# Adaptive-norm modulation in four column groups of TensorE, in plain float32

## The chip, the cores and the metric

One core of a Trainium2 chip runs the kernel. The metric is the device time of one execution in microseconds, the median over several runs. The profile is of one execution; its clock starts with the first instruction on the core.

## What is computed

The kernel is one inference step of a one-layer hybrid decoder: 1024 prompt positions and 8 sequences of 4 new positions, 1056 rows of width 1024. The part that is changed is the modulation, a small product of the 9 conditioning vectors (1 prompt, 8 samples) with a wide weight:

```python
mod = (jax.nn.silu(c) @ p['w_mod'] + p['b_mod'])[:, None, :]
sh_m, sc_m, g_m, sh_f, sc_f, g_f = jnp.split(mod, 6, axis=-1)
h = rmsnorm(x, p['g_pre_mix']) * (1.0 + sc_m) + sh_m
z = h @ p['w_in']
...
x = x + g_m * rmsnorm(merged @ p['w_out'], p['g_post_mix'])
hf = rmsnorm(x, p['g_pre_ffn']) * (1.0 + sc_f) + sh_f
```

`w_mod` is 1024 x 6144 in float32. The first third of `mod` (`sh_m`, `sc_m`) is needed before the first product `h @ w_in` can begin; the rest only after the branches (convolution, S5 state space, attention) have been merged.

## The kernel before, in words

All weights come from memory in float32. A large product is done three times in the fast format fp32r: each weight tile is split into a rounded part `whi` (ScalarE, L414) and a remainder `wlo` (VectorE, L415), the data likewise into `hh` and `hl`, and TensorE runs `whi*hh`, `whi*hl`, `wlo*hh`. Plain float32 operands need no split; TensorE then runs each matmul as two passes, which the trace shows as two MATMUL rows.

The order of the work is a list of atoms. An atom is a piece of TensorE work (for a 128-column weight tile: three atoms, one for each 352 of the 1056 rows, 24 matmuls each) with the weight units it needs, an assumed cost in microseconds, and an evacuation of PSUM that is issued after the next atom's matmuls. `run` (L370) walks over the list. Before an atom it issues splits (`split`, L397) of the units that `ready` lets through, and loads (`load`, L382) up to three units ahead. `Side` (L218) holds generators for the work beside the products (convolution taps on VectorE, attention, the sample's attention, layer norm, S5). After each atom `side.advance(cost)` lets every generator go on by that cost, so the generators' instructions stand between the atoms according to assumed costs and not to measured time. `side.finish` and `side.drain` issue whatever is left of a generator at once, with no atom between.

The modulation is cut into 12 column blocks `n` of 512 columns, each into 4 units `kk` of 128 x (2 x 512) weights (512 KB).

- Blocks 0 to 3 are made first (`first_mod`, L540): 16 units through 6 buffers `mw`, two plain float32 matmuls a unit with a stationary of 9 columns (`cs1`) and 512 moving columns. Block `n` is turned from rows to columns by `turn_mod` (4 transposes) while block `n+1` is running. Between these units, in TensorE's program order, stand the statistics of the first two thirds of `x` (`first_stats`: 4 matmuls of one column, then a Newton root on VectorE ending in `rs_dg`) and their broadcast (`first_norm`).
- Blocks 4 to 11 (32 units) are atoms among the products (`mod_atoms`, L568; `add_mod`, L599, cost 0.9). Their weights are split like all others. A unit has four fp32r matmuls of 18 stationary columns (`c18`, rounded part and remainder of the conditioning) by 512. At a block's end ScalarE copies 18 x 512 out of PSUM into a part of `vm` (L574), TensorE transposes it in four pieces (L576), VectorE adds the parts.

`some_mods(n)` puts the next `n` units into the list: one after each q and k tile, one after each conv half and gate tile, through the 11 tiles up to and after the S5 input.

In attention `value` (L849) multiplies by head with output in partitions 0 to 63 or 64 to 127; its program order is pair, head, key block, so that with two key blocks two matmuls (four passes) for one head stand before two for the other. In S5 (`s5_gen`, L1260), for each of 4 quarters, `Gin` times `U` alternates matmul by matmul between the halves of the partitions; ScalarE copies the result `E`, VectorE scans it and builds `HP`, and TensorE multiplies `Tm` by `U` and `Go` by `HP`. When the list comes to `open_m(0)` (L1728), `side.finish` issues what is left of S5.

Of the kernel before, what the change touches and what calls it, by code (L numbers as in the profile page):

```python
# [8 lines left out]
F32 = mybir.dt.float32  # L9
# [41 lines left out]
V_CB, V_LG, V_LB, V_CW = 80, 84, 88, 92  # L51
NVEC = 92 + 124
C_ID, C_ONE = 0, 128
NCST = 256

# [16 lines left out]
def _constants():  # L74
    f = np.float32
    cst = np.zeros((128, NCST), f)
    cst[:, C_ID:C_ID + 128] = np.eye(128)
    cst[:, C_ONE:C_ONE + 128] = 1.0
    sel = np.zeros((12, 6, 128), f)
    for gp in range(6):  # L80
        for m in range(128):
            sel[4 * (gp // 2) + 2 * (gp % 2) + m // 64, gp, m] = 1.0
    slopes = np.exp2(f(-8.0) * np.arange(1, NSLOPE + 1, dtype=f) / f(NSLOPE)).astype(f)
    tab = np.full((128, 2560), BIG, f)
    qi = np.arange(128)[:, None]
    ki = np.arange(256)[None, :]
    dist = qi + 128 - ki
    ok = (dist >= 0) & (dist <= 128)
    for g in range(2):
        for h in range(4):  # L90
            t = slopes[4 * g + h] * (DIL[g] * dist).astype(f)
            tab[:, (4 * g + h) * 256:(4 * g + h + 1) * 256] = np.where(ok, t, f(BIG))
    i2 = np.arange(128)
    dist2 = i2[:, None] - i2[None, :]
    ok2 = (dist2 >= 0) & (dist2 % 2 == 0)
    for h in range(4):
        t = slopes[8 + h] * (8 * dist2).astype(f)
        tab[:, 2048 + h * 128:2048 + (h + 1) * 128] = np.where(ok2, t, f(BIG))
    smp = np.full((128, 992), BIG, f)
    for b in range(8):  # L100
        for h in range(4):
            for j in range(4):
                r = b * 16 + h * 4 + j
                m = np.arange(512)
                d = 512 + j - m
                smp[r, 0:512] = np.where((d % 4 == 0) & (d <= 512), slopes[4 + h] * d.astype(f), f(BIG))
                m = np.arange(128)
                d = 128 + j - m
                smp[r, 512:640] = np.where(d <= 128, slopes[h] * d.astype(f), f(BIG))
                m = (np.arange(64)[:, None] * 16 + np.arange(4)[None, :]).reshape(-1)  # L110
                d = 1024 + j - m
                smp[r, 640:896] = np.where(d % 16 == 0, slopes[8 + h] * d.astype(f), f(BIG))
                for g in range(3):
                    for j2 in range(4):
                        if j2 == j or (g == 0 and j2 < j):
                            smp[r, 896 + g * 32 + b * 4 + j2] = slopes[4 * g + h] * f(j - j2)
    return cst, sel, tab, smp
# [138 lines left out]
def program(tc, I, O):  # L256
# [113 lines left out]
    def run():  # L370
# [11 lines left out]
        def load(v):  # L382
            src, n, scale, op, keep = units[v]
            if op:
                op['load']()
                return
            raw = wp.tile([128, 1024], F32, tag="raw", name="raw")
            sp.dma_start(out=raw[:, 0:n], in_=src)
            raws[v] = raw
# [7 lines left out]
        def split(v):  # L397
            src, n, scale, op, keep = units[v]
            for t in tags(v):
                rings[t].append(v)  # L400
            if op:
                flush()
                if v + 1 < len(units) and units[v + 1][3]:
                    units[v + 1][3]['pre']()
                parts[v] = wp.tile([128, 1024], F32R, tag=tags(v)[0], name="wop")
                op['make'](parts[v])
                return
            raw = raws.pop(v)
            if keep:
                hi, lo = keep()  # L410
            else:
                hi = wp.tile([128, 1024], F32R, tag="whi", name="whi")
                lo = wp.tile([128, 1024], F32R, tag="wlo", name="wlo")
            act.activation(out=hi[:, 0:n], in_=raw[:, 0:n], func=AF.Copy, scale=scale)  # L414
            dve.scalar_tensor_tensor(out=lo[:, 0:n], in0=raw[:, 0:n], scalar=scale, in1=hi[:, 0:n].bitcast(F32),  # L415
                                     op0=ALU.mult, op1=ALU.subtract)
            parts[v] = (hi, lo)

        def ready(v, i):
            if any(len(rings[t]) >= 3 and last[rings[t][-3]] >= i for t in tags(v)):  # L420
                return False
            ahead = 6 if units[v][3] else 2
            return v < ahead or first[v - ahead] <= i

        def loadable():
# [76 lines left out]
    ks_ = sc_.tile([128, 3, 2, 32], F32, name="ks_")  # L502
    vm = sc_.tile([128, 768], F32, name="vm")
    vs_ = vm[0:32].rearrange("p (g x) -> p g x", g=3)
    mrow = vm[64:82, 0:512]
    cvp_, close_cv = open_pool("cv", side="right", bufs=1)
    mp, close_mp = open_pool("mp", side="right", bufs=1)
    cT = mp.tile([128, 8, 9], F32, name="cT")
# [22 lines left out]
    act.activation(out=cth, in_=cT, func=AF.Tanh, scale=0.5)  # L531
    cs2 = mp.tile([128, 8, 9], F32, name="cs2")
    dve.scalar_tensor_tensor(out=cs2, in0=cth, scalar=1.0, in1=cT, op0=ALU.add, op1=ALU.mult)
    c18 = sc_.tile([128, 8, 18], F32R, name="c18")
    act.activation(out=c18[:, :, 0:9], in_=cs2, func=AF.Copy)
    TT(c18[:, :, 9:18], cs2, c18[:, :, 0:9].bitcast(F32), ALU.subtract)
    cs1 = mp.tile([128, 8, 9], F32, name="cs1")
    dve.tensor_scalar(out=cs1, in0=cs2, scalar1=0.5, scalar2=None, op0=ALU.mult)

    def first_mod(n, kk):  # L540

        def emit(_):
            if kk == 0:
                mws['s', n] = zt()
            s = mws['s', n]
            i = 4 * n + kk
            w = mws.pop(i)
            for k2 in range(2):
                k = kk * 2 + k2
                mm(s[0:9, :], cs1[:, k, :], w[:, k2 * 512:(k2 + 1) * 512], k == 0, k == 7)  # L550
            load_mw(i + 6)
            if kk == 1 and n:
                turn_mod(n - 1)

        def finish(_):
            mws['row', n] = mp.tile([9, 512], F32, tag="row", name="row", bufs=2)
            act.activation(out=mws['row', n], in_=mws['s', n][0:9, :], func=AF.Copy)
        atoms.append(Atom([], 1.7, emit, finish if kk == 3 else None))

    def turn_mod(n):  # L560
        row = mws.pop(('row', n))
        s = mws.pop(('s', n))
        for i in range(4):
            pe.transpose(out=s[:, i * 9:(i + 1) * 9], in_=row[:, i * 128:(i + 1) * 128], identity=ident[0:9, 0:9])
        TT(mod[:, 4 * n:4 * n + 4, :], s[:, 0:36].rearrange("p (i x) -> p i x", i=4),
           vecs[:, V_BMOD + 4 * n:V_BMOD + 4 * n + 4].unsqueeze(2).to_broadcast([128, 4, 9]), ALU.add)

    def mod_atoms(n):  # L568

        box = {}  # L570

        def finish(_):
            s = box['s']
            act.activation(out=mrow, in_=s[0:18, :], func=AF.Copy)  # L574
            for i in range(4):
                pe.transpose(out=s[:, i * 18:(i + 1) * 18], in_=mrow[:, i * 128:(i + 1) * 128],  # L576
                             identity=ident[64:82, 64:82])
            t3 = s[:, 0:72].rearrange("p (i x) -> p i x", i=4)
            tm = sc_.tile([128, 4, 9], F32, tag="mtm", name="mtm", bufs=2)
            TT(tm, t3[:, :, 0:9],  # L580
               vecs[:, V_BMOD + 4 * n:V_BMOD + 4 * n + 4].unsqueeze(2).to_broadcast([128, 4, 9]), ALU.add)
            TT(mod[:, 4 * n:4 * n + 4, :], tm, t3[:, :, 9:18], ALU.add)

        out = []
        for kk in range(4):
            def emit(w, kk=kk):
                if kk == 0:
                    box['s'] = mt()
                s = box['s']
                hi, lo = w[0]  # L590
                for k2 in range(2):
                    k = kk * 2 + k2
                    mm(s[0:18, :], c18[:, k, :], hi[:, k2 * 512:(k2 + 1) * 512], k == 0, False)
                    mm(s[0:18, :], c18[:, k, :], lo[:, k2 * 512:(k2 + 1) * 512], False, k == 7)
                return None
            out.append((flat(I['wmod'][n, kk]), emit, finish if kk == 3 else None))
        return out

    def add_mod(m):  # L599
        if atoms[-1].tag == 'mod' and atoms[-1].evac:  # L600
            plain(lambda: None)
        u = unit(m[0], 1024, 0.5)
        atoms.append(Atom([u], 0.9, m[1], m[2], tag='mod'))

    hpool, close_h = open_pool("hpool", bufs=1)
    hh = hpool.tile([128, 8, T], F32R, name="hh")
# [499 lines left out]
    def s5_prep():  # L1106
# [73 lines left out]
        yield 2.0  # L1180
        tmp1, tmp2 = t16(), t16()

        PW = sc_.tile([128, 2, 9, 16], F32, name="PW")
        dve.memset(PW[:, 0, 0, :], 1.0)
        dve.memset(PW[:, 1, 0, :], 0.0)
        TT(PW[:, 0, 1, :], mag, co, ALU.mult)
# [41 lines left out]
        yield 2.0  # L1228
        cmul_small(5, 4, 4)

        WK = sc_.tile([128, 7, 2, 16], F32, name="WK")

        def csq(orr, oi, ar, ai):
            TT(tmp1, ai, ai, ALU.mult)
# [427 lines left out]
    for g in range(3):  # L1662
        for what, base, scale in (('Q', 12, -0.125), ('K', 18, 1.0)):
            for p in range(2):
                put(z_atoms(base + 2 * g + p, scale, qk_evac(g, what, p)))
                some_mods(1)
        if g == 0:
            conv_job(1, 1)
            conv_start(1)
# [2 lines left out]
        plain(lambda g=g: P_.update({('gen', g): side.add(att_gen(g))}))  # L1672
        if g < 2:
            conv_job(g + 2, 1)
        gate_jobs(GA[g], 1)
        if g < 2:
            conv_start(g + 2)
        plain(lambda: None)
        plain(lambda g=g: side.finish(P_['gen', g]))
    plain(lambda: (P_.update(cg=side.add(combine_gen())), side.add(s5_prep())))  # L1680
    gate_jobs(GC, 1)
    plain(lambda: (side.finish(P_['cg']), P_['close_ap'](), close_cv(), open_ub(), side.add(ln_gen()),
                   side.add(sample_gen())))
    gate_jobs(GS, 0)
# [737 lines left out]
```

## Time and profile before

| what | before |
|---|---|
| median of 3 runs | 1982.06 us (1979.92 to 1983.1) |
| the profiled execution | 1981.16 us |
| span of its instructions | 1979.4 us |
| TensorE busy | 1890.1 us, 95% |
| VectorE busy | 1339.0 us, 68% |
| ScalarE busy | 735.7 us, 37% |
| mean granted TensorE clock | 0.976 |

The span is the time from the first instruction on the core to the last; 1.8 us of the execution lie outside it. Busy time counts an engine's own instructions; matmuls overlap, and their ends are modelled, so what a matmul costs in a row of matmuls is read from the distance of starts.

### The profile page before, as it was taken

How to read it: one execution, taken by the hardware profiler on the slowest of the kernel's cores; microseconds unless marked ns; L12 is line 12 of the kernel's file. 1: busy time of each engine (PE TensorE's matmuls, PEld its weight loads, DVE VectorE, ACT ScalarE, POOL GpSimd, SP SyncE). 2: the span in 40 equal slices, each digit the busy share in tenths (PEclk: the TensorE clock that was granted, in tenths of full speed). 3: DMA queues.
4: the chain of work that ended last, by engine and by line, in shares of the span. 5: the costliest groups of instructions: out<-in, count | busy, mean ns of one | idle time of the engine just before them, and what ended most of it. 6: DMA issues, size and time to landing. Idle time of an engine off the chain costs nothing. (4 is left out here: it accounts for less than half of the span.)

```text
span 1979.4 us, 33713 instructions
## 1 busy us (share of the span) xinstructions
PE 1890.1 (95%) x13512; PEld 1761.9 (89%) x13512; DVE 1339.0 (68%) x2747; ACT 735.7 (37%) x1442; POOL 230.2 (12%) x385
## 2 busy tenths in 40 slices
PE   7999999999999899999899999999999999999995
PEld 2899799789777789999799999989999999999995
DVE  5777686465366676665596667777777777667686
ACT  3422422431531443222223446434333333464452
POOL 0000001001010023122200001100000000110123
PEclk9999999999999999999999999999999999999997
DMA  7333124224237453233852345541423223575654
GB/s 287 96 107 111 47 107 151 67 97 165 86 123 282 166 177 124 92 116 95 238 158 89 106 153 196 207 167 67 133 85 109 82 88 119 200 266 182 218 196 152
DMA packets 89261, 282.23 MB, mean 143 GB/s; under 512 B 16004, under 2 KB 22244, under 8 KB 86928
## 3 DMA queue, kind: packets, MB, share of 16 engines
q1 hardware_dynamic: 51824, 138.49, 21.6%
q0 software_dynamic: 29936, 115.11, 16.7%
q10 hardware_dynamic: 7344, 26.47, 4.0%
q8 instruction: 106, 1.74, 0.4%
q14 instruction: 51, 0.42, 0.1%
HBM read 212.80 MB, written 68.15 MB: 142 GB/s over the span
## 5 line engine op out<-in xcount | busy, mean ns | idle before, releaser
L307 PE MATMUL z<-mh,wop 128*128 128x264 f32 x2032 | 395.8, 287 | 4.3 <-ACT wop L2042 2.8
L307 PE MATMUL z<-hh,whi 128*128 128x352 f32 x1152 | 380.1, 330 | 3.2 <-ACT whi L414 1.8
L307 PE MATMUL z<-hh,wlo 128*128 128x352 f32 x1152 | 373.0, 324 | 3.1 <-DVE wlo L415 3.1
L307 PE MATMUL z<-hl,whi 128*128 128x352 f32 x1152 | 373.1, 324 | 0.8 <-DVE hl L310 0.8
L307 PE MATMUL z<-ml,wop 128*128 128x264 f32 x1400 | 342.1, 286 | 7.1 <-DVE ml L310 7.0
L307 PEld LDWEIGHTS z<-mh,wop 128*128 128x128 f32 x2032 | 327.5, 191 | 6.3 <-ACT wop L2042 3.3
L415 DVE SCALAR_TENSOR_TENSOR wlo<-raw,whi 128x1024 fp32r<-128x1024 f32 x132 | 160.9, 1222 | 146.3 <-ACT whi L414 145.2
L307 PEld LDWEIGHTS z<-ml,wop 128*128 128x128 f32 x1400 | 243.0, 190 | 8.0 <-DVE ml L310 7.9
L307 PEld LDWEIGHTS z<-hh,whi 128*128 128x128 f32 x1152 | 218.9, 190 | 15.3 <-issue 7.0
L307 PEld LDWEIGHTS z<-hh,wlo 128*128 128x128 f32 x1152 | 218.8, 190 | 3.7 <-DVE wlo L415 3.7
L307 PEld LDWEIGHTS z<-hl,whi 128*128 128x128 f32 x1152 | 219.0, 190 | 2.7 <-DVE hl L310 1.7
L414 ACT ACTIVATE whi<-raw 128x1024 fp32r<-128x1024 f32 x132 | 139.2, 1056 | 180.8 <-PE z L307 166.1
L1529 DVE SCALAR_TENSOR_TENSOR ycv<-cub,vecs,ycv 128x1024 f32<-128x1024 f32 x120 | 153.9, 1282 | 3.1
L2042 ACT ACTIVATE wop<-raw 128x512 fp32r<-128x512 f32 x150 | 91.2, 616 | 145.1 <-PE z L307 118.2
L307 PE MATMUL z<-xa,wop 128*128 128x264 f32 x792 | 108.2, 285 | 0.7 <-DVE wop L2046 0.7
L307 PEld LDWEIGHTS z<-xa,wop 128*128 128x128 f32 x792 | 100.9, 189 | 1.0 <-DVE wop L2046 0.9
L310 DVE TENSOR_TENSOR wop<-raw,wop 128x512 fp32r<-128x512 f32 x90 | 61.9, 688 | 44.5 <-ACT wop L2042 44.5
L307 PE MATMUL z<-mh,whi 128*128 128x264 f32 x288 | 85.8, 298 | 0.8 <-DVE ft L310 0.6
L307 PE MATMUL z<-ml,whi 128*128 128x264 f32 x288 | 83.1, 289 | 0.0
L307 PE MATMUL z<-mh,wlo 128*128 128x264 f32 x288 | 82.8, 288 | 0.0
L307 PE MATMUL z<-zh,whi 128*128 128x264 f32 x256 | 73.6, 287 | 0.0
L307 PE MATMUL z<-zl,whi 128*128 128x264 f32 x256 | 72.8, 284 | 0.0
(437 smaller groups left out, 3712.7 us busy)
## 6 DMA issues: line engine op xcount, KB each, us to landing
raw<-i_win SPq DMA_DIRECT2D x48, 512.0 KB, 3.7
raw<-i_wfi SPq DMA_DIRECT2D x43, 512.0 KB, 4.1
raw<-i_wfo SPq DMA_DIRECT2D x80, 256.0 KB, 3.3
fd<-ft POOLq DMA_DIRECT2D x22, 792.0 KB, 6.9
raw<-i_wmod SPq DMA_DIRECT2D x32, 512.0 KB, 4.4
gd<-g ACTq DMA_DIRECT2D x24, 528.0 KB, 2.9
g<-gd ACTq DMA_DIRECT2D x24, 528.0 KB, 4.7
ml<-fd POOLq DMA_DIRECT2D x22, 528.0 KB, 6.7
```

Of the source, the lines that this page charges most:

```text
L307: return pe.matmul(out=out, lhsT=lhsT, rhs=rhs, start=start, stop=stop, **kw)
L310: dve.tensor_tensor(out=out, in0=a, in1=b, op=op)
L414: act.activation(out=hi[:, 0:n], in_=raw[:, 0:n], func=AF.Copy, scale=scale)
L415: dve.scalar_tensor_tensor(out=lo[:, 0:n], in0=raw[:, 0:n], scalar=scale, in1=hi[:, 0:n].bitcast(F32), op0=ALU.mult, op1=ALU.subtract)
L1529: dve.scalar_tensor_tensor(out=a_, in0=ub[:, k:k + TP], scalar=wv[:, k:k + 1], in1=a_, op0=ALU.mult, op1=ALU.add)
L2042: act.activation(out=w[:, 0:n], in_=src, func=AF.Copy, scale=scale)
```

## The change

- `mod_mm` takes the place of both kinds of matmul. A unit is now four plain float32 matmuls of 32 stationary columns (9 of them used) and 256 moving columns. Each writes to its own 32 partitions of PSUM: the two halves of the 512 columns times the two halves of the unit's 256 inputs. So it uses four different column groups of the array.
- The four groups are added afterwards: a block's 128 x 256 result is copied to SBUF by one ScalarE instruction, and two float32 matmuls with a constant 0/1 matrix (`C_SUM`, 18 columns) add the groups and turn them at the same time (`mod_turn`); one VectorE instruction adds the bias.
- The 32 later units are no longer split. Their weights are loaded as they are straight into a buffer of the `whi` or the `wlo` ring, by a DMA that `split` issues; `load` does nothing for them.
- Their assumed cost falls from 0.9 to 0.3, and they stand earlier: two after each q and k tile and each of the first gate tiles, none in the gates before S5 (`gate_jobs(GC, 0)`) and so none left for the S5 stretch.
- `c18` and `mrow` go; `PW` and `WK` of S5 share a tile `pw` with the copy.

```diff
+    for r in range(4):
+        for i in range(9):
+            cst[32 * r + i, C_SUM + 9 * (r // 2) + i] = 1.0
...
+            if op and op.get('asis'):
+                parts[v] = wp.tile([128, 1024], F32, tag=tags(v)[0], name="wmo")
+                sp.dma_start(out=parts[v], in_=src)
+                return
...
-            ahead = 6 if units[v][3] else 2
+            ahead = 6 if units[v][3] and not units[v][3].get('asis') else 2
...
+    def mod_mm(s, w, kk):
+        for half in range(2):
+            for k2 in range(2):
+                r, k = 64 * half + 32 * k2, kk * 2 + k2
+                c0 = k2 * 512 + half * 256
+                mm(s[r:r + 32, 0:256], cs1[:, 9 * k:9 * k + 32], w[:, c0:c0 + 256], kk == 0, kk == 3)
+
+    def mod_turn(n, s, row):
+        for i in range(2):
+            mm(s[:, 256 + i * 18:256 + (i + 1) * 18], row[:, i * 128:(i + 1) * 128], cst[:, C_SUM:C_SUM + 18], True, True)
...
-            for k2 in range(2):
-                k = kk * 2 + k2
-                mm(s[0:9, :], cs1[:, k, :], w[:, k2 * 512:(k2 + 1) * 512], k == 0, k == 7)
+            mod_mm(mws['s', n], mws.pop(i), kk)
...
-                for k2 in range(2):
-                    k = kk * 2 + k2
-                    mm(s[0:18, :], c18[:, k, :], hi[:, k2 * 512:(k2 + 1) * 512], k == 0, False)
-                    mm(s[0:18, :], c18[:, k, :], lo[:, k2 * 512:(k2 + 1) * 512], False, k == 7)
+                mod_mm(box['s'], w[0], kk)
...
-        u = unit(m[0], 1024, 0.5)
-        atoms.append(Atom([u], 0.9, m[1], m[2], tag='mod'))
+        u = unit(m[0], 1024, 1.0, dict(asis=True, no=nmod[0], ahead=3))
+        nmod[0] += 1
+        atoms.append(Atom([u], 0.3, m[1], m[2], tag='mod'))
...
-                some_mods(1)
+                some_mods(2)
...
-        gate_jobs(GA[g], 1)
+        gate_jobs(GA[g], 2)
...
-    gate_jobs(GC, 1)
+    gate_jobs(GC, 0)
```

How the instructions stand. TensorE, the first modulation (`mw` are the weights, `s` the statistics and broadcast), before:

```order
L307 MATMUL z<-mw,cs_120 9x512 x10
L307 MATMUL s<-cst,sq 88x1 x4
L307 MATMUL z<-mw,cs_120 9x512 x2
L564 MATMUL z<-cst,row 128x9 x4
L307 MATMUL z<-mw,cs_120 9x512 x2
L307 MATMUL s<-rs_dg,cst 128x352
L307 MATMUL z<-mw,cs_120 9x512 x6
L564 MATMUL z<-cst,row 128x9 x4
L307 MATMUL z<-mw,cs_120 9x512 x6
L307 MATMUL s<-cst,sq 88x1 x4
```

and in the changed kernel:

```order
L311 MATMUL z<-mw,cs_118 32x256 x20
L311 MATMUL s<-cst,sq 88x1 x4
L311 MATMUL z<-mw,cs_118 32x256 x4
L311 MATMUL z<-cst,row 128x18 x2
L311 MATMUL z<-mw,cs_118 32x256 x4
L311 MATMUL s<-rs_dg,cst 128x352
L311 MATMUL z<-mw,cs_118 32x256 x12
L311 MATMUL z<-cst,row 128x18 x2
L311 MATMUL z<-mw,cs_118 32x256 x12
L311 MATMUL s<-cst,sq 88x1 x4
```

The places are the same; each unit has four short matmuls in place of two long ones, and a turn two in place of four.

TensorE after the first q tile (`m` is the modulation's PSUM tile, `wmo` its unsplit weights), before:

```order
L307 MATMUL z<-hh,wlo 128x352
L307 MATMUL m<-whi,c_117 18x512
L307 MATMUL m<-wlo,c_117 18x512
L307 MATMUL m<-whi,c_117 18x512
L307 MATMUL m<-wlo,c_117 18x512
L307 MATMUL z<-hh,whi 128x352
```

and in the changed kernel:

```order
L311 MATMUL z<-hh,wlo 128x352
L311 MATMUL m<-wmo,cs_118 32x256 x8
L311 MATMUL z<-hh,whi 128x352
```

One unit before, two units at one place now. Over the whole list there are 13 such places with two units and 6 with one, and the last lies before the attention of the third head group.

ScalarE at the end of S5 (`E` copies the last quarter's scan input, each `g` empties one atom of a gate tile, `ysb` copies the result of `Tm` and `HP`), before:

```order
L1379 ACTIVATE E<-s 128x2x144 x4
L414 ACTIVATE whi<-raw 128x1024
L1611 ACTIVATE g<-z 128x352
L1613 DMA gd<-g 128x1056
L1611 ACTIVATE g<-z 128x352 x3
L1613 DMA gd<-g 128x1056
L1441 ACTIVATE ysb<-s 128x3x136 x2
```

and in the changed kernel:

```order
L1386 ACTIVATE E<-s 128x2x144 x4
L1618 ACTIVATE g<-z 128x352 x2
L1620 DMA gd<-g 128x1056
L1448 ACTIVATE ysb<-s 128x3x136 x2
```

A gate atom is emptied one atom late, so three atoms stood between `E` and the last `Tm` product before, and one stands there now. The split `whi<-raw` that stood behind `E` now stands ahead of it.

## Rows read from the trace of the kernel before

**Rows 1.** The page, part 1: busy time, share, instructions of each engine.
```profile
PE 1890.1 (95%) x13512; PEld 1761.9 (89%) x13512; DVE 1339.0 (68%) x2747; ACT 735.7 (37%) x1442; POOL 230.2 (12%) x385
```
**Rows 2.** Busy time by stretch (stretch, length, engines, PEclk, DMA share, GB/s), at the start.
```profile
25.00:30.00 5.00, 5.00 (x16) 1.15 (x14) 2.49 (x3) 2.68 (x2) 0.00 (x0) 1.00 0.92 342
...
35.00:40.00 5.00, 5.00 (x16) 1.27 (x15) 3.46 (x16) 2.32 (x4) 0.00 (x0) 1.00 0.34 105
...
45.00:50.00 5.00, 4.15 (x15) 3.59 (x16) 3.80 (x8) 4.09 (x7) 0.00 (x0) 0.66 0.73 249
```
**Rows 3.** Timeline of PE at the start (start, length, instruction, count, idle before).
```profile
28.32 5.32 PE L307 MATMUL z<-mw,cs 128*9 128x512 f32 x12
33.57 0.79 PE L307 MATMUL s<-cst,sq 128*88 128x1 f32 x8
...
39.05 1.89 PE L307 MATMUL z<-mw,cs 128*9 128x512 f32 x4
```
**Rows 4.** Timeline of ACT at the start.
```profile
25.15 2.53 ACT L656 ACTIVATE sq<-xc 128x2816 f32<-128x2816 f32 x1
```
**Rows 5.** Timeline of DVE at the start.
```profile
28.61 3.10 DVE L310 TENSOR_TENSOR sq<-sq 128x1408 f32<-128x1408 f32 x3
34.40 0.16 DVE L465 TENSOR_SCALAR rs_v<-s 88x4 f32<-88x4 f32 x1 [2.68 <-PE s L307]
...
37.45 0.20 DVE L616 SCALAR_TENSOR_TENSOR Aq<-mod,vecs 128x36 f32<-128x36 f32 x1
```
**Rows 6.** Timeline around the first later unit.
```profile
101.26 0.32 PE L307 MATMUL z<-hh,wlo 128*128 128x352 f32 x1
...
101.42 0.39 PE L307 MATMUL m<-whi,c 128*18 128x512 f32 x1
...
102.35 0.32 PE L307 MATMUL z<-hh,whi 128*128 128x352 f32 x1
```
**Rows 7.** Timeline of PE around one `Gin` times `U` of S5.
```profile
758.11 0.32 PE L307 MATMUL z<-hh,wlo 128*128 128x352 f32 x1
758.37 2.18 PE L307 MATMUL s<-U,Gin 128*64 128x144 f32 x32
760.48 0.43 PE L307 MATMUL z<-hh,whi 128*128 128x352 f32 x1
760.74 0.32 PE L307 MATMUL z<-hl,whi 128*128 128x352 f32 x1
```
**Rows 8.** Timeline of PE around one `value` of attention.
```profile
248.96 1.15 PE L307 MATMUL s<-PT,V 128*64 128x128 f32 x16
250.04 0.27 PE L859 MATMUL s<-cst,stt 128*8 128x128 f32 x1
```
**Rows 9.** Waits of PE, 50 to 1000 us (waiter, awaited: sum, times, longest).
```profile
PE s L307 <- ACT vh L1004: 4.9, 3, 2.3
PE m L576 <- ACT vm L574: 3.6, 3, 1.6
```
**Rows 10.** The page, part 5: the splits (count, busy, mean ns, idle before).
```profile
L415 DVE SCALAR_TENSOR_TENSOR wlo<-raw,whi 128x1024 fp32r<-128x1024 f32 x132 | 160.9, 1222 | 146.3 <-ACT whi L414 145.2
...
L414 ACT ACTIVATE whi<-raw 128x1024 fp32r<-128x1024 f32 x132 | 139.2, 1056 | 180.8 <-PE z L307 166.1
```
**Rows 11.** Timeline of PE at the end of S5 and behind it.
```profile
926.63 2.18 PE L307 MATMUL s<-U,Gin 128*64 128x144 f32 x32
940.29 0.39 PE L307 MATMUL s<-U,Tm 128*128 128x136 f32 x2
...
954.88 0.66 PE L307 MATMUL z<-at_h,whi 128*128 128x352 f32 x1 [2.68 <-DVE mrg L1764]
```
**Rows 12.** Timeline of DVE at the end of S5.
```profile
929.30 0.69 DVE L310 TENSOR_TENSOR f<-E,WT 128x512 f32<-128x512 f32 x1 [5.75 <-ACT E L1379]
...
931.24 1.22 DVE L415 SCALAR_TENSOR_TENSOR wlo<-raw,whi 128x1024 fp32r<-128x1024 f32 x1
...
940.25 0.69 DVE L310 TENSOR_TENSOR HP<-HP,m 128x512 f32<-128x512 f32 x1
```

More of the change, by code (lines that the diff above doesn't have):

```diff
@@ L53 @@
 C_ID, C_ONE = 0, 128
-NCST = 256
+C_SUM = 256
+NCST = C_SUM + 18
 def _tiles(w, kt, n):
@@ L384, in load @@
             if op:
-                op['load']()
+                if not op.get('asis'):
+                    op['load']()
                 return
@@ L504, in program @@
     vs_ = vm[0:32].rearrange("p (g x) -> p g x", g=3)
-    mrow = vm[64:82, 0:512]
+    pw = sc_.tile([128, 512], F32, name="pw")
     cvp_, close_cv = open_pool("cv", side="right", bufs=1)
@@ L533, in program @@
     dve.scalar_tensor_tensor(out=cs2, in0=cth, scalar=1.0, in1=cT, op0=ALU.add, op1=ALU.mult)
[L534 to L538, printed above, removed]
+    cs1 = sc_.tile([128, 96], F32, name="cs1")
+    dve.memset(cs1[:, 72:96], 0.0)
+    dve.tensor_scalar(out=cs1[:, 0:72], in0=flat(cs2), scalar1=0.5, scalar2=None, op0=ALU.mult)
+    def mod_mm(s, w, kk):
[7 more added lines that the diff above has]
+            mm(s[:, 256 + i * 18:256 + (i + 1) * 18], row[:, i * 128:(i + 1) * 128], cst[:, C_SUM:C_SUM + 18], True, True)
+        TT(mod[:, 4 * n:4 * n + 4, :].rearrange("p (h i) x -> p h i x", h=2),
+           s[:, 256:292].rearrange("p (i h x) -> p h i x", i=2, h=2),
+           vecs[:, V_BMOD + 4 * n:V_BMOD + 4 * n + 4].rearrange("p (h i) -> p h i", h=2).unsqueeze(3).to_broadcast(
+               [128, 2, 2, 9]), ALU.add)
     def first_mod(n, kk):
@@ L544, in emit @@
                 mws['s', n] = zt()
-            s = mws['s', n]
             i = 4 * n + kk
-            w = mws.pop(i)
-            for k2 in range(2):
-                k = kk * 2 + k2
-                mm(s[0:9, :], cs1[:, k, :], w[:, k2 * 512:(k2 + 1) * 512], k == 0, k == 7)
+            mod_mm(mws['s', n], mws.pop(i), kk)
             load_mw(i + 6)
@@ L555, in finish @@
         def finish(_):
-            mws['row', n] = mp.tile([9, 512], F32, tag="row", name="row", bufs=2)
-            act.activation(out=mws['row', n], in_=mws['s', n][0:9, :], func=AF.Copy)
+            mws['row', n] = mp.tile([128, 256], F32, tag="row", name="row", bufs=2)
+            act.activation(out=mws['row', n], in_=mws['s', n][:, 0:256], func=AF.Copy)
         atoms.append(Atom([], 1.7, emit, finish if kk == 3 else None))
     def turn_mod(n):
[L561 to L566, printed above, removed]
+        mod_turn(n, mws.pop(('s', n)), mws.pop(('row', n)))
     def mod_atoms(n):
@@ L572, in finish @@
         def finish(_):
[L573 to L582, printed above, removed]
+            row = pw[:, 0:256]
+            act.activation(out=row, in_=box['s'][:, 0:256], func=AF.Copy)
+            mod_turn(n, box['s'], row)
         out = []
@@ L588, in emit @@
                     box['s'] = mt()
-                s = box['s']
-                hi, lo = w[0]
-                for k2 in range(2):
-                    k = kk * 2 + k2
-                    mm(s[0:18, :], c18[:, k, :], hi[:, k2 * 512:(k2 + 1) * 512], k == 0, False)
-                    mm(s[0:18, :], c18[:, k, :], lo[:, k2 * 512:(k2 + 1) * 512], False, k == 7)
+                mod_mm(box['s'], w[0], kk)
                 return None
@@ L597, in mod_atoms @@
         return out
+    nmod = [0]
     def add_mod(m):
@@ L1181, in s5_prep @@
         tmp1, tmp2 = t16(), t16()
-        PW = sc_.tile([128, 2, 9, 16], F32, name="PW")
+        assert not mods
+        PW = pw[:, 0:288].rearrange("p (r s t) -> p r s t", r=2, s=9)
         dve.memset(PW[:, 0, 0, :], 1.0)
@@ L1229, in s5_prep @@
         cmul_small(5, 4, 4)
-        WK = sc_.tile([128, 7, 2, 16], F32, name="WK")
+        WK = pw[:, 288:512].rearrange("p (i r t) -> p i r t", i=7, r=2)
         def csq(orr, oi, ar, ai):
```

## The prediction

> **What bounds the kernel now.** I read the page's first part first. TensorE is busy 95% of the span, VectorE 68%, ScalarE 37% [rows 1]. So the time is TensorE's own work plus the few places where it waits, and work taken from another engine counts only where TensorE waits for it. The change removes 64 splits, 32 of 1.06 us on ScalarE and 32 of 1.22 us on VectorE, 34 and 39 us. But the idle time ahead of these rows is nearly all a wait for TensorE (166.1 of 180.8 us) or for the partner split (145.2 of 146.3) [rows 10]: they run ahead of TensorE and are covered by its atoms. By themselves I count them at nothing. The cover is the tile ahead of each, which stays.
>
> Then I read the windows and the timelines of the start, where no products run yet, of one later unit, and of S5's end; and the waits, to see where TensorE is late at all.
>
> **Term 1, the front: -2.8 us.** The 12 passes from 28.32 to 33.57 us cost 5.25/12 = 0.4375 us each for 512 columns [rows 3]. A unit has four, 1.75 us. With four groups at once it has 8 passes of 256 columns, each 0.219 us: 0.44 us a unit. TensorE's work of the first 16 units falls from 28 to 7 us. That is no gain of 21, because the weights still have to come: at 25 to 30 us the DMA share is 0.92 at 342 GB/s, and TensorE is busy throughout; at 35 to 40 us the DMA share is only 0.34 [rows 2]. So the loads are through shortly after 30 us, while TensorE's last modulation row ends at 39.05 + 1.89 = 40.94 [rows 3]. What is late next are the statistics. ScalarE's square ends at 25.15 + 2.53 = 27.68 [rows 4]; VectorE's sum starts at 28.61 and ends at 31.71 [rows 5]; TensorE takes it at 33.57 only, behind the units that stand ahead of it [rows 3], and the Newton root on VectorE starts at 34.40 after waiting 2.68 us for TensorE [rows 5]. In the changed kernel TensorE waits for that sum instead. It gains 33.57 - 31.71 = 1.9 us, and the sum itself can start 0.9 us earlier (28.61 - 27.68), since the bias addition ahead of it no longer waits for a late turn: 2.8 us. The bounds are 0 (a chain on VectorE that I do not see) and -8 (the front follows the loads: from 40.94 to about 33).
>
> **Term 2, the later 32 units: -9.3 us.** Before, a unit costs 102.35 - 101.42 = 0.93 us of TensorE [rows 6], in all 29.8. No row shows four groups of the array at work, so I bound it. Nothing overlapping is 8 x 0.219 = 1.75 a unit; two at a time 0.875; four 0.44. The nearest rows are those of S5: 32 `Gin` passes of 144 columns, alternating between two groups. One alone would be 0.4375 x 144/512 = 0.123. From the product ahead of them to the second one behind them are 760.74 - 758.11 = 2.63 us [rows 7]; two products are spaced 0.16 [rows 6], so with two passes at a time I expect 0.16 + 16 x 0.123 + 0.16 = 2.29. Two groups overlap in full, and the visit costs 0.34 besides. `value` in attention is the second near row: 16 passes of 128 columns take 250.04 - 248.96 = 1.08 us [rows 8], where one alone would be 0.109 and eight slots 0.87, though program order puts four passes of one group ahead of four of the other. So TensorE also finds overlap that does not stand next to each other. In the change, the two passes of one matmul share a group and the next matmul has another; I take four at a time. There are 19 visits (13 of two units, 6 of one): 32 x 0.4375 + 19 x 0.34 = 20.5, against 29.8.
>
> **Term 3, the ends of the blocks: -2.5 us.** TensorE waits 3.6 us in three places for the copy `vm` ahead of its turn [rows 9]. With the changed places of the units a tile's atom stands between copy and turn, so most of it goes; bounds 0 and -3.6. The copy and the two matmuls of a turn otherwise replace a copy and four transposes of about the same length: nothing, either way.
>
> **Term 4, the end of S5: +6.3 us.** Here the change takes cover away. No unit is left for the gates, so the generator of S5 has fewer atoms and is finished at once with one atom in place of three between the last `Gin` and the last `Tm`. What must happen in between: `Gin` ends at 926.63 + 2.18 = 928.81 [rows 11], then ScalarE's copy and VectorE's scan from 929.30 to `HP` at 940.25 + 0.69 = 940.94 [rows 12]: 12.1 us. A split of 1.22 us in the middle [rows 12] now stands ahead of it, which leaves 10.9. Before, `Tm` came at 940.29 [rows 11], behind three atoms, so nothing was lost. Now one atom of 24 x 0.16 = 3.84, the switch of 0.34 and `Tm` itself, 0.39 [rows 11], stand against the 10.9: a wait of 6.3 us. All that follows S5 comes that much later. Bounds: 0 if the generator's steps fall earlier than the assumed costs say, +8 if the split stays in the chain.
>
> **Term 5, cover lost elsewhere: +1.9 us.** A unit among the gates gave 0.93 us in which side work went on. Where TensorE already waits for side work (4.9 us for `vh` in three places [rows 9]), a unit gone from there lengthens the wait by as much: two such places, 1.9; bounds 0 and +5. At 954.88 TensorE waits 2.68 us for VectorE's `mrg` [rows 11]; it stays.
>
> **Term 6, the clock: +0.9 us.** Around 45 to 50 us the granted clock is 0.66 in the mean, so about 3.4 of the 5 us ran at 1.2 GHz instead of 2.4 [rows 2], behind a stretch in which TensorE waited. One such stretch more costs at most half of it, 1.7 us of work; with the front idler now I take half of that. Bounds 0 and +3.4.
>
> **Queues.** The load of a unit into the `whi` or `wlo` ring is issued on SP when `split` comes to it, and it waits there until TensorE has read the ring's old tile. Behind it in SP's queue stands the raw load of a next tile. A tile is 72 matmuls x 0.16 = 11.5 us, and loads are issued up to three units ahead, so both still come in time: nothing. If that lead were gone, each double place would wait for a DMA; this is part of the fourth rival. On POOL nothing is moved past anything.
>
> **Sum.** -2.8 - 9.3 - 2.5 + 6.3 + 1.9 + 0.9 = -5.5. The profiled execution took 1981.16 us, which gives 1975.7. It stands 0.9 below the median of the runs, so the forecast is 1976.6. About 0.2% (4.0 us) is what a measurement can tell from no change, so faster means below 1978.1 and slower above 1986.0.
>
> **Rivals.**
>
> *The groups do not run four at a time (slower).* Place: every later unit. At two at a time a unit is 0.875 us: 32 x 0.4375 = 14.0 us more than forecast, 1990.6. It decides the sign from 5.5/32 = 0.17 us more a unit, 0.61 us, or fewer than 2.9 groups at work. A harder form: if passes start and end strictly in program order, the two passes of one group follow each other and only the last pass of one group and the first of the next lie together: 5 slots x 0.219 = 1.09 us, 21 us over the forecast, 1997.6. By the same order `value` would have 13 slots of 0.109, 1.42 us, and it took 1.08 [rows 8], so the row speaks against it. The Trainium skill (TensorE: Matmul & The Clock Gate, Part 3, "What overlaps and what doesn't") has such a rule: matmuls are strict FIFO, and a weight load overlaps matmuls in flight only where its row group differs, which here it never does, as all four use the full rows. By that rule the change would be slower; the row contradicts it for two groups, and no row shows four. The same section's table has three column groups 2.38 times as fast as one; at that rate for each group, an estimate, a unit would be 0.55 us and the time about 1980. Chance 0.12: 0.07 for two at a time, 0.05 for strict order.
>
> *The lost cover eats the gain (no change).* Terms 4 and 5 at their upper ends, 8 and 5: -2.8 - 9.3 - 2.5 + 8 + 5 + 0.9 = -0.7, or 1981.4 beside the median; with a front that gains nothing as well 1984.2. For it: VectorE's chain in S5 is a chain of single instructions with no slack. Against it: two bad ends have to come together. Chance 0.22.
>
> *The front follows the loads, and S5 is covered (much faster).* Term 1 at -8, term 4 at +3: 8.5 us more gain, 1968.1. For it: the DMA share of 0.34 [rows 2]. Against: the statistics come from VectorE, not from the weights. Chance 0.13.
>
> *The loads are late.* The raw tiles wait behind a unit's load, and TensorE behind both. It would show as waits for DMA in the q and k tiles; 13 places at an assumed 0.5 us each give 1983.1, within the second rival's range, and I count it there.
>
> **Chances and range.** The forecast has 0.53, with its own range 1970 to 1981. About 0.08 of it lies above 1978.1. Faster: 0.45 + 0.13 = 0.58. Slower: 0.12 + 0.04 of the lost cover's case = 0.16. No change: 0.08 + 0.18 = 0.26. The range of 1966 to 1986 leaves out the groups' case (0.12) and 0.04 on either side.
>
> **What would show it.** Right: the 8 passes of 256 columns start within about 0.44 us of product time; a double visit lasts 0.9 + 0.34 from the product ahead to the one behind; the second statistics start near 30.7 in place of 33.57; the wait for `vm` is gone; a wait of some 6 us for `HP` stands at the last `Go`. Wrong: a double visit of 2 us or more (the rival of the groups); the last modulation row of the front still near 40 us; no wait at S5's end, or one over 8 us; waits of products for weight loads in the q and k tiles.

## The result, and the profile after

The changed kernel took 2000.47 us in the median of 4 runs (1997.97 to 2005.93), the kernel before 1980.99 (1979.43 to 1983.1) beside it: a ratio of 1.0101, 95% interval 1.008 to 1.0122. It is 1% slower, 19.5 us; forecast were 5.5 us faster. The profiled execution took 2002.44 us, with a span of 2000.7.

Part 1 of the page, as in [rows 1]:

```profile
PE 1881.1 (94%) x13704; PEld 1767.0 (88%) x13704; DVE 1301.0 (65%) x2707; ACT 700.7 (35%) x1409; POOL 230.4 (12%) x385
```

TensorE's busy time fell by 9.0 us, VectorE's by 38, ScalarE's by 35, and the time rose by 19.5. So what came in is not more work; it is waiting, and work at a lower clock. The timeline of TensorE shows the parts of the change at their places (start, length, instruction, count, idle time before and what ended it):

```profile
31.55 0.76 PE L311 MATMUL s<-cst,sq 128*88 128x1 f32 x8 [2.64 <-DVE sq L314]
...
39.51 0.66 PE L311 MATMUL z<-hh,whi 128*128 128x352 f32 x1
...
98.78 0.32 PE L311 MATMUL z<-hh,wlo 128*128 128x352 f32 x1
99.03 1.07 PE L311 MATMUL m<-wmo,cs 128*32 128x256 f32 x16
100.03 0.43 PE L311 MATMUL z<-hh,whi 128*128 128x352 f32 x1
...
276.85 0.66 PE L311 MATMUL z<-hh,wlo 128*128 128x352 f32 x1 [4.88 <-DVE wlo L424]
...
943.86 0.47 PE L311 MATMUL s<-U,Tm 128*128 128x136 f32 x2 [0.67 <-ACT g L1618]
948.38 0.79 PE L311 MATMUL s<-HP,Go 64*128 64x136 f32 x2 [4.06 <-DVE HP L314]
```

The statistics start at 31.55 in place of 33.57 [rows 3], and wait now. The first product starts at 39.51; the same product stood at 42.6 before. Two units cost 100.03 - 98.78 - 0.16 = 1.09 us, so the four groups do work together: 16 passes that would take 16 x 0.219 = 3.5 us alone are through in 1.00. The waits for `wlo` and `HP` further down are new; so is what follows them. The windows (stretch, length, engines, PEclk, DMA share, GB/s):

```profile
270.00:285.00 15.00, 10.12 (x56) 9.03 (x56) 7.93 (x9) 1.38 (x4) 0.00 (x0) 0.77 0.48 167
...
725.00:740.00 15.00, 13.39 (x62) 12.75 (x63) 8.89 (x49) 3.39 (x7) 5.46 (x11) 0.66 0.32 101
...
940.00:950.00 10.00, 4.45 (x25) 3.69 (x23) 9.86 (x22) 0.46 (x1) 1.65 (x4) 0.92 0.65 197
950.00:970.00 20.00, 19.78 (x66) 16.02 (x67) 4.00 (x15) 2.65 (x5) 4.29 (x8) 0.53 0.33 98
```

From 950 to 970 us TensorE is busy, at a granted clock of 0.53 in the mean: nearly all of it at 1.2 GHz, right behind the stretch in which it was busy for 4.45 of 10 us. Summed over the span, TensorE had 130.7 us at half clock in this execution, 93.1 in the first profile of the kernel before. In the second profiles of both, which come with the experiments, it was 108.2 and 86.4: part of the difference is one between executions.

To see where the time went, both traces are cut at the same products, and the lengths between them compared. The first column names the cut by its time before. "Waits" sums TensorE's idle gaps over 0.15 us; "half clock" is half of the time at 1.2 GHz outside the waits; "units" is the time from the start of each matmul of a later unit or turn to the start of the next matmul, without waits (the first 16 units, in the first row, are not in it). All are differences to the first profile of before, in us. The second profile of the kernel before differs from the first by up to 2.7 us in one stretch, so single figures of that size say little.

| stretch | after | units | waits | half clock | after, 2nd | lead | lead, 0.9 | single |
|---|---|---|---|---|---|---|---|---|
| to 42.6 | -3.0 | – | +9.4 | +2.1 | -2.6 | -2.8 | -2.8 | -2.2 |
| 42.6 to 264.8 | +1.3 | -1.0 | +0.6 | -1.0 | +1.5 | +3.4 | -0.8 | -2.2 |
| 264.8 to 344.1 | +12.0 | +0.7 | +6.6 | +2.9 | +12.0 | +1.3 | +1.3 | -0.6 |
| 344.1 to 716.1 | -5.6 | -9.0 | +1.3 | -0.6 | -5.8 | -4.4 | -4.9 | -2.7 |
| 716.1 to 991.1 | +8.9 | -6.4 | +4.6 | +11.3 | +5.7 | +9.0 | +5.8 | -3.6 |
| 991.1 to 1735 | +0.5 | 0 | +1.5 | -1.7 | +1.1 | +1.1 | +1.1 | +0.8 |
| 1735 to the end | +7.3 | 0 | +5.6 | +1.9 | +4.5 | +5.0 | +2.1 | +6.3 |

The last four columns are the profiles of experiments told below. The change saves 16 us of units and turns. Two stretches take 21 us (18 in the second profile): around 270 us, and S5 with its end. The last one, where the change touches nothing, takes some more.

### The profile page after: what moved, and what is told of

The parts are those of the page before. It is cut to its first block, busy times and chain, and to the rows that moved or that the text cites. A ratio compares the mean times of both kernels' runs of the same rounds, so it can differ in the third digit from the quotient of the medians.

```text
span 2000.7 us, 33966 instructions
## 1 busy us (share of the span) xinstructions
PE 1881.1 (94%) x13704; PEld 1767.0 (88%) x13704; DVE 1301.0 (65%) x2707; ACT 700.7 (35%) x1409; POOL 230.4 (12%) x385
## 5 line engine op out<-in xcount | busy, mean ns | idle before, releaser
L311 PE MATMUL z<-mh,wop 128*128 128x264 f32 x2032 | 398.3, 288 | 10.7 <-ACT wop L2049 4.5
L311 PE MATMUL z<-hh,whi 128*128 128x352 f32 x1152 | 384.5, 334 | 3.0 <-ACT whi L423 1.5
L424 DVE SCALAR_TENSOR_TENSOR wlo<-raw,whi 128x1024 fp32r<-128x1024 f32 x100 | 122.0, 1222 | 115.5 <-ACT whi L423 114.6
L423 ACT ACTIVATE whi<-raw 128x1024 fp32r<-128x1024 f32 x100 | 105.1, 1055 | 107.7 <-PE z L311 94.5
L834 ACT ACTIVATE P<-P,stt 128x128 f32<-128x128 f32 (+1 forms) x96 | 42.1, 439 | 89.9 <-DVE stt L831 89.9
```

Source lines behind the costliest of these rows:

```text
L311: return pe.matmul(out=out, lhsT=lhsT, rhs=rhs, start=start, stop=stop, **kw)
L834: act.activation(out=P[:, h, 0:nk], in_=P[:, h, 0:nk], func=AF.Exp, scale=-1.0, bias=stt[:, b, hd:hd + 1], accum_out=stt[:, b, 4 + hd:5 + hd])
```

## The experiments

Theory 1: the arithmetic is sound, and the loss is one of order. Two units at one place take the lead from the splits; an assumed cost of 0.3 in place of 0.9 shifts the side work against the products; S5 without units has too little cover at its end. Rivals: the arithmetic itself costs (a lower clock, loads in the way), or VectorE's chains are late in any order. Each result is given as its ratio to the kernel before on the same chip, with the 95% interval.

**The lead of the splits.** A split is let through when the unit two places ahead of it starts. With q tile, unit, q tile that is the tile ahead; with two units between, it is the first unit, just ahead of the use. On VectorE of the changed kernel, around the wait of 4.88 us:

```profile
270.24 0.27 DVE L878 COPY ST<-s 8x128 f32<-8x128 f32 x1
270.44 5.22 DVE L1536 SCALAR_TENSOR_TENSOR ycv<-cub,vecs,ycv 128x1024 f32<-128x1024 f32 x4
275.58 1.22 DVE L424 SCALAR_TENSOR_TENSOR wlo<-raw,whi 128x1024 fp32r<-128x1024 f32 x1
```

The split stands behind four more convolution taps of 1.3 us, and TensorE behind the split. The edit:

```diff
-            return v < ahead or first[v - ahead] <= i
+            p = v - ahead
+            if not units[v][3]:
+                while p > 0 and (units[p][3] or {}).get('asis'):
+                    p -= 1
+            return v < ahead or first[p] <= i
```

> The changed kernel; unsplit units no longer count in the rule by which a split may run ahead, so the split of the tile behind a double place is issued when the tile ahead of it begins, as in the kernel before. Theory 1 (the double places took the lead from the splits): TensorE's waits for wlo between 250 and 350 us, 6.0 + 2.4 us in the changed kernel, go, and with them the stretch at half clock behind the longest: 8 to 11 us less than the changed kernel, about 1990. Rival (VectorE's taps are late by themselves, the split only stands in their queue): the wait moves to the next product or tap, and the time stays within 3 us of the changed kernel's 2000.

Measured: 1990.89 us, ratio 1.0045 (1.0029 to 1.006). VectorE now, with the taps behind the split:

```profile
270.94 0.27 DVE L882 COPY ST<-s 8x128 f32<-8x128 f32 x1
271.14 1.20 DVE L424 SCALAR_TENSOR_TENSOR wlo<-raw,whi 128x1024 fp32r<-128x1024 f32 x1
272.27 5.22 DVE L1540 SCALAR_TENSOR_TENSOR ycv<-cub,vecs,ycv 128x1024 f32<-128x1024 f32 x4
```

TensorE's waits of 250 to 350 us, four for `wlo` with 6.9 us in the changed kernel, are gone, the half clock of 276 to 283 us with them, and the stretch 264.8 to 344.1 falls from +12.0 to +1.3. Theory 1 holds here; the wait did not move to another product of this stretch.

**The end of S5.** The edit lowers the assumed costs of S5's steps, so that its work is issued earlier:

```diff
-SY = 1.0
+SY = 0.96
```

> The changed kernel with the assumed costs of S5's steps at 0.96 of theirs, which puts three atoms in place of one between the last Gin and the last Tm, as before the change. Theory 1 (lost cover at the end of S5, and the half clock behind it): the waits for HP and g there, 4.2 + 1.3 + 0.8 us, go, and most of the 20 us at half clock behind them: 10 to 14 us less than the changed kernel, 1986 to 1990. Rival (the chain on VectorE is the bound whatever stands between): the wait moves to mrg behind S5, the gain is under 3 us.

Measured: 1997.86, ratio 1.0074 (1.0058 to 1.0089), 3 to 5 us less than the changed kernel (by its ratios of 1.0087 in a second measurement, below, and 1.0101) and not 10 to 14. The intervals overlap, so the times alone do not prove a gain. The waits of TensorE from 920 us on, first of the changed kernel, then of this one:

```profile
PE s L311 <- DVE HP L314: 5.1, 2, 4.1
PE z L311 <- DVE mrg L1771: 5.0, 5, 1.9
PE s L311 <- ACT g L1618: 0.7, 1, 0.7
```

```profile
PE z L311 <- DVE mrg L1771: 11.4, 7, 5.1
```

The wait for `HP` is gone, and 6.4 us more for `mrg`, the next thing behind S5 (VectorE joins the branches with their gates `g` there), stand in its place.

What the edit does gain lies in the row of matmuls that ends S5, `Tm` and `Go` in turn, 48 MATMUL rows up to the first product behind it. That product starts, before and in the changed kernel, at:

```profile
949.03 0.43 PE L307 MATMUL z<-at_h,whi 128*128 128x352 f32 x1
```

```profile
964.64 0.66 PE L311 MATMUL z<-at_h,whi 128*128 128x352 f32 x1
```

Before, the row took 949.03 - 940.29 [rows 11] = 8.7 us, at full clock. In the changed kernel it took 964.64 - 943.86 = 20.8 us, 5.1 of them waits for `HP`, so 15.7 for the same matmuls. The clock fell at the wait and rose at 968.8 us only, behind the first products. With the edit the row is back at 8.7 us. All five profiles of this study with waits for `HP` have a row of 14.3 to 15.7 us beside the waits; without them it is 8.7 (before, with this edit, with both edits, and with single places). So at this place a wait costs 6 to 7 us beside itself.

Over the whole stretch from 716 us on, 17.1 us at half clock are left of 34.1 in the first profile of the changed kernel. Of these 17 us, 6.8 are a difference around 730 us which the second profile of the changed kernel has too, without the edit. The rival was mostly right: three atoms of cover at this place do not buy what they seemed to, because the wait for `mrg` takes much of it back.

**Both together.**

> Both edits together. Theory 1: the gains add, 18 to 25 us less than the changed kernel, 1975 to 1982, at or below the kernel before. Rival (the shorter work on TensorE only shows the next chain): less than 12 us, above 1988.

Measured: 1985.99, ratio 1.0008 (0.9996 to 1.002): no different from the kernel before, 16 to 18 us less than the changed kernel. The two gains (8 to 11 and 3 to 5 us by their ratios) add, within the noise; the expected 1975 to 1982 was missed from above.

**The arithmetic with the places of before.** One unit stands at each place, also among the gates and in S5. There the tile `pw` cannot be shared with S5 any more, so `PW` and `WK` have tiles of their own again, and the copy of a block is made by two ScalarE instructions into two small tiles. The lines that set places and cost:

```diff
-        atoms.append(Atom([u], 0.3, m[1], m[2], tag='mod'))
+        atoms.append(Atom([u], 0.9, m[1], m[2], tag='mod'))
...
-                some_mods(2)
+                some_mods(1)
...
-        gate_jobs(GA[g], 2)
+        gate_jobs(GA[g], 1)
...
-    gate_jobs(GC, 0)
+    gate_jobs(GC, 1)
```

> The arithmetic of the change (four groups, unsplit weights, the new front) with the places and the assumed cost 0.9 of the kernel before: one unit at each place, gates and S5 included; the copy of a block goes in two halves into two tiles. Theory 1 (the loss is one of placement): 32 units at about 0.66 us in place of 0.93 give 9 us, the front 3, the waits for vm 2 to 3: 1966 to 1970. Rival (the arithmetic itself costs: the granted clock falls because TensorE has less to do, or the unsplit loads disturb the others): 1985 or more, with a mean clock of 0.97 or less and the same 7 us more in the last 250 us as in the changed kernel.

Measured: 1975.55, ratio 0.996 (0.9945 to 0.9975): faster than the kernel before by 7 to 8 us, the best kernel of the study. The mean granted clock is 0.975, and the S5 stretch is 3.6 us shorter than before instead of 8.9 longer. The rival of a costly arithmetic falls. The expected 1966 to 1970 was missed by some 6 us; the last row of the table has 6.3 us that theory 1 did not count.

**The assumed cost alone.** From that kernel, 0.9 to 0.3 and to 1.2, and S5's costs to 0.96:

```diff
-        atoms.append(Atom([u], 0.9, m[1], m[2], tag='mod'))
+        atoms.append(Atom([u], 0.3, m[1], m[2], tag='mod'))
```

> The kernel with one unit at each place, with the assumed cost of a unit at 0.3 as in the change in place of 0.9. Nothing else differs; two atoms in place of three stand between the last Gin and the last Tm. Theory 1 (the assumed cost sets how much cover a step gets): a wait of 2 to 4 us for HP returns and with it a stretch at half clock, 4 to 10 us slower than with 0.9: 1980 to 1986. Rival (only the places matter): within 2 us of 1975.5.

Measured: 1991.72, ratio 1.0034 (1.0014 to 1.0053). The number alone takes back the whole gain and as much again, some 15 us by the two ratios. In its profiled execution (a span of 1984.7, the shortest of the five) two waits for `HP` return, 2.0 us in all, and the row that ends S5 takes 14.3 us beside them in place of 8.7: the S5 stretch has 17 us more at half clock than with 0.9. The median is above the expected 1980 to 1986.

> The kernel with one unit at each place, with the assumed cost at 1.2 in place of 0.9. Theory 1 (the rest of the program is paced for 0.9, and either side of it loses cover somewhere): 3 to 10 us slower than with 0.9. Rival (a larger cost gives the side work a larger share, the more the better): 1970 to 1975.

Measured: 1981.12, ratio 0.999 (0.9978 to 1.0001): also slower than with 0.9, as theory 1 expected.

> The kernel with one unit at each place and cost 0.9, with S5's assumed costs at 0.96. Theory 1 (S5 has its cover already): no more than 2 us either way, 1974 to 1977. Rival (S5's end still waits for mrg, 2.5 us): 2 to 4 us faster, 1972 to 1973.

Measured: 1983.13, ratio 1.0005 (0.999 to 1.002): neither expectation. S5 is finished some 3 us earlier, and VectorE's timeline shows what that meets:

```profile
956.39 1.38 DVE L1772 SCALAR_TENSOR_TENSOR mrg<-g,z 128x352 f32<-128x352 f32 x3 [9.90 <-DMA g<-gd]
960.40 1.02 DVE L1772 SCALAR_TENSOR_TENSOR mrg<-g,z 128x352 f32<-128x352 f32 x2 [2.62 <-DMA g<-gd]
```

The gates `g` come back from memory late. The DMA issues of 935 to 965 us (count, KB each, median us to landing) in this kernel, then of 925 to 965 us in the one with S5's costs at 1.0:

```profile
g<-gd ACTq DMA_DIRECT2D x5, 528.0 KB, 14.3
```

```profile
g<-gd ACTq DMA_DIRECT2D x8, 528.0 KB, 7.8
```

The two windows are not alike; the first three gate loads alone took 14.3, 17.8 and 19.7 us here, against 4.9, 7.5 and 10.2 us. Two things stand ahead of them that came otherwise with S5's costs at 1.0. S5's store `yd` and its first five loads `yq` are issued before the first gate load, where they came behind the second and the third one. And three loads `cc_l`, of 528 KB each, are issued within 1.1 us before the first gate load, where they had a lead of some 8 us. TensorE waits 15.6 us for `mrg`. So an earlier end of S5 changes which transfers share the DMA engines; which of the two made the gates late was not tested.

**Lead and cost together, double places kept.**

```diff
-        atoms.append(Atom([u], 0.3, m[1], m[2], tag='mod'))
+        atoms.append(Atom([u], 0.9, m[1], m[2], tag='mod'))
```

on top of the first experiment, with the changed kernel run beside it.

> The changed kernel with the lead of the splits restored (as in the first experiment) and the assumed cost of a unit at 0.9 as before the change; the double places and the S5 stretch without units stay. Theory 1 (pace and cover both count, and S5 still has one atom of cover): 2 to 6 us less than with the lead alone, 1984 to 1990, the wait for HP still there. Rival (the assumed cost is all that the lead does not explain): 1976 to 1980, like the kernel with single places.

> The changed kernel once more, on the chip and in the call of the next three, so that they can be compared with it directly. 1.0 to 1.2% over the kernel before; the waits for wlo between 250 and 350 us and for HP at the end of S5 at the same places as in its first profile.

Measured: the changed kernel 2000.33, ratio 1.0087 (1.0062 to 1.0112), a little under the expected 1.0 to 1.2%, with the waits for `wlo` and `HP` at the same places; with lead and cost 1983.37, ratio 1.0005 (0.9987 to 1.0022), just below the expected 1984 to 1990. The wait for `HP` is still there:

```profile
934.62 0.79 PE L311 MATMUL s<-HP,Go 64*128 64x136 f32 x2 [4.16 <-DVE HP L314]
```

So of the 25 to 28 us between the changed kernel and the one with single places, the lead is worth about 9, the assumed cost about 8 more, and the places themselves (units left among the gates and in S5) about 9, taken in this order: in the table S5 is 5.8 us longer than before with lead and cost, 3.6 shorter with the single places.

**The front, and the last 250 us.** In all kernels with the new front the end, from 1735 us on, is 2 to 7 us longer than in the first profile of before. Three runs looked for the reason: the kernel before with the new front alone, the kernel before again, and the kernel before with 18 unused columns in its constants, so that the tiles behind them lie as with the new ones.

```diff
-NCST = 256
+NCST = 256 + 18
```

> The kernel before with the new front alone (blocks 0 to 3 in four column groups); the later units as they were. Theory 1 (the front gains at the first product and gives part back at half clock): the first product 2 to 3 us earlier, about 1 us left at 100 us, 1 to 2 us in all, which is within what can be told from no change. Rival for the last 250 us, where all four kernels so far lost 5 to 7 us against the profile of before though nothing there is changed: if the new front alone (with its 18 constants more) shows that loss too, it comes with the changed layout or the earlier start and not with the later units.

> The kernel before once more, for a second profile. Theory 1 for the end (the loads of the last 250 us land differently from execution to execution): its waits after 1730 us differ from the first profile by some us, up to the 5 to 7 of the changed kernels. Rival (something in the changed kernels makes them late): they agree within 1 us.

> The kernel before with 18 unused columns more in its constants, which moves all tiles behind them by 72 bytes; no instruction differs. Theory 1 for the last 250 us: the layout has nothing to do with it, waits there and the time agree with the kernel before within 2 us. Rival: the layout makes the loads there late, 5 us more from 1870 us on, as in the kernel with the new front alone.

Measured: the front alone 1981.14, ratio 0.9986 (0.9974 to 0.9998), so 0.4 to 5 us faster; the kernel before 1982.06 in one run, with an end 0.9 us shorter than in its first profile; the unused columns 1984.19, ratio 1.0007 (0.9995 to 1.002), with an end 0.8 us longer. The 18 columns are not the reason, nor is it a matter of executions of the kernel before: its two profiles agree within 1 us there, as the rival had it. With the front alone the end is 4.3 us longer. What makes it so stays open: TensorE's waits there for `wop` and `mh`, operands of the last products, are 10.9 us in that trace in place of 5.0, but why an earlier start should change that was not found.

## Why the prediction was wrong

- **The bound** was read rightly: work taken from VectorE and ScalarE (38 and 35 us) gained nothing by itself. The sentence that failed stands behind it: "The cover is the tile ahead of each, which stays." It does not stay. The rule that lets a split run ahead counts units, and two unsplit units use up its count. That place alone cost 12 us in the stretch 264.8 to 344.1, and restoring the lead took 10.7 of them back.
- **Queues**: "nothing" was right for the loads (no wait for a later unit's weights is in the trace) and wrong for what the text set beside them, the lead of the next split on VectorE. With four taps of 1.3 us ahead of it in VectorE's order, the split came 5 us late, with its raw weights in SBUF since 258 us.
- **Term 1**, -2.8: the first product came 3.05 us earlier (2.3 with the front alone), and the front alone gave 2.8 by its ratio, with an interval of 0.4 to 5. Right. The statistics waited for the sum on VectorE, as forecast.
- **Term 2**, -9.3: two units 1.09 us in place of the 1.21 forecast; 13 such visits and 6 single ones at 0.66 make 18.1 against 29.8, or -11.7. Right, and a little better than forecast: a visit costs 0.22 us beside its passes and not 0.34. The trace records four passes starting within 20 ns of each other and the next four 0.22 us later. The rival's harder form, which the prediction set beside the rule that matmuls run strictly in order and weight loads overlap them only across row groups (the Trainium skill, TensorE: Matmul & The Clock Gate, Part 3), would have had 2.2 us for two units, and measured were 1.09. So read, the rule does not hold for four column groups here; what it says of the order of whole matmuls these rows do not decide.
- **Term 3**, -2.5: no wait for the copy of a block is left among the later units. Right.
- **Term 4**, +6.3: 5.1 us for `HP` and 0.7 for `g`. Right as a wait, but not as a price: 20.5 us at half clock followed it, in which the row that ends S5 took 15.7 us in place of 8.7. And giving the cover back did not cure it, since `mrg` is late behind it too.
- **Term 5**, +1.9: the wrong place. The waits for `vh`, which it made longer, fell from 4.9 us in three places to 3.3. What cost time in its stead was the assumed cost of a unit, which the sum did not price at all and which moves all side work against the products: 8 us in the double kernel, and 15 in the single one by its ratios.
- **Term 6**, +0.9: the term that was most mis-sized. Outside the front the half clock cost 13 us more than before in the first profile and 6 in the second. Some 3 us of it follow the wait for `wlo`, and 7 lie in the row behind the wait for `HP`, so it should have been priced with the waits.
- **The rivals**: the slower one had the wrong mechanism (the groups do work four at a time). The nearest one, lost cover, had one of the two places, the end of S5, and its upper ends lay only 5 us over the forecast, 8 with a front that gains nothing; the two stretches took 21.

That the kernel with single places, at 1975.55 us, lies near the forecast of 1976.6 is luck. That kernel has the gains of terms 1 to 3, 14.6 us by the forecast, without the lost cover of terms 4 and 5, and gained 7 to 8; the last 250 us, which no term has, took 6.3 back in its profile.

## What to carry to other kernels

Where an order is written for assumed costs, a cheaper instruction is a change of the order: keep the places and the costs that the rest was arranged for, measure, and move things afterwards one at a time. Rules that count units ("two ahead") must count the units that they were meant for; a new kind of unit in the list uses up their lead. A wait of TensorE is to be priced with the work that then runs at half clock: here 3 us behind the wait of 4.9 us for `wlo`, 7 us behind those of 5.1 us for `HP`, and 5.6 us at the same place behind waits of 2.0 us only.

## What was not expected of the hardware

Four plain float32 matmuls with 32 stationary columns each, in four column groups, do run as the prediction had assumed from rows that showed two at most: 16 passes of 256 columns in 1.00 us. Not expected was that the row of short matmuls that ends S5, once begun at half clock, ran at it to its end: 15.7 us beside the waits, in place of 8.7. And the first three gate loads of 528 KB took 14 to 20 us where `yd`, five `yq` and three `cc_l` had been issued just ahead of them, 5 to 10 us in the kernel in which `yd` and `yq` came among or behind them and the `cc_l` long before.
